# A feed-forward's first output part by block products, with modulation rows moved and the mixer's end list-scheduled

## The chip, the cores and the metric

The kernel runs on one core of one Trainium2 chip. The metric is the device time of one execution in microseconds (us). The runs of the kernel before took 983.15, 978.13 and 983.17 us, a median of 983.15.

## The reference

One decoder layer over 512 tokens of width 1024, in float32. Nine vectors of 1024 values (shift, scale and gate for each of three sub-layers) are made from a conditioning vector: `mod = silu(c) @ w_ada + b_ada`. Then:

```python
u = modulate(rmsnorm(h, g_norm_ffn1), sh1, sc1)
h = h + 0.5 * gt1 * swiglu(u, w_ffn1_in, w_ffn1_out)
u = modulate(rmsnorm(h, g_norm_mix), sh2, sc2)
h = h + gt2 * token_mixing(u, ...)
u = modulate(rmsnorm(h, g_norm_ffn2), sh3, sc3)
h = h + 0.5 * gt3 * swiglu(u, w_ffn2_in, w_ffn2_out)
out = rmsnorm(h, g_final)
```

`swiglu(u, w_in, w_out)` is `(silu(u @ w_a) * (u @ w_b)) @ w_out` with an inner width of 2816, that is 22 tiles of 128. `token_mixing` projects `u`, pools and attends, and ends with `merged = sigmoid(gates_1) * (y_pool @ w_pb) + sigmoid(gates_2) * (y_attn @ w_ab)` and `merged @ w_out`.

## The kernel before

**Precision.** Each float32 matrix product is made of three matmuls on a pair of float32r tiles, a leading part and a remainder (`mm3`): hi x hi, hi x lo, lo x hi. Leading parts are made by ScalarE (a copy), remainders by VectorE (a subtraction). This holds for activations (`UH`/`UL`, `HI`/`HK`) and for weights: every weight chunk of 128 x 1024 is loaded by SP into a raw buffer, and `split_hi` and `split_lo` write it into the rings `whi` and `wlo`, some chunks ahead of its use (`look`, `take`). For chunks in the set `added`, the remainder is made by ScalarE (a negated copy) and an adding DMA issued by GpSimd, and VectorE is spared.

**Layout.** Tokens are columns, 512 of them (`T`, half of it `HT`); features are tiles of 128 rows. The residual is `H[0..7]`.

**Feed-forward.** The 22 inner tiles are worked in five parts, `PARTS = ((0, 4), (4, 8), (8, 12), (12, 16), (16, 22))`. For each part the inner activations of its tiles are made, and then the part's share of the output is added to `H`. An inner tile is made in one of two ways. *Plain* (`ffn_pair`): two tiles of 24 matmuls of 512 columns (one for `a`, one for `b`), a silu and a product. *By blocks* (`duo`): two inner tiles at once, as a 2 x 2 block product with seven products instead of eight (Winograd's form of Strassen's scheme); each product is 24 matmuls of 256 columns. The output of a part has the same two ways: plain, 8 tiles of 4 x 3 matmuls of 512 columns; or by `out_block`, seven products of 24 matmuls of 256 columns. For `out_block` the activations of four inner tiles are needed as seven blocks: `split_a` splits two blocks that are there, `split_s` makes four sums of 256 columns and splits them. Of a part's four output chunks, three more weight blocks are sums; VectorE (`make`) and GpSimd (`sum`, an adding DMA) make them in the buffers `X`.

`BLOCKED = (1, 2, 3)` says for which parts the output is by `out_block`, in both feed-forwards. In the second one (`ffn2`) pairs 0 to 3 are plain (`PLAIN[2] = 4`): two in `head`, beside the norm, two behind it. Then comes part 0's plain output, then part by part two duos and an output block.

**Modulation rows.** One row is a column of `mod` for 128 features: SP loads 512 KB of `wada`, and VectorE multiplies by the condition and sums (`ada_do`). `bg()` does one row and starts the next load. Rows 56 to 63 run in the mixer's output loop, rows 64 to 71 (half of the last gate) in the second feed-forward, from its head to pair 3, with the buffers `cs` and `AR`.

**Order.** Between `begin()` and `end()` the calls go to a `Recorder`. `flush` then issues them: TensorE's in the written order, those of the other engines, SP and GpSimd included, by a list schedule with estimated costs and due times. Both feed-forwards are recorded. The mixer is not: its calls are issued as written, the gates (`gate_duo`), the branches (`branch`) and the output loop of `merge_out` and its tail (`out_tail`) included. In the gates' blocks, `branch`'s `merge` and `parts` wait in the list `rest` and are put by hand between the products.

**Lines.** Recorded instructions all carry line 320 (`flush`). Written ones carry their own: 521 and 538 the weight splits, 599 the rows, 664 to 674 the norm's statistics and their spread, 681 to 707 the norm, 730 and 731 the tail.

Of the kernel before, what the change touches and what calls it, by code (L numbers as in the profile page):

```python
# [14 lines left out]
P = 128  # L15
# [3 lines left out]
KT = 8  # L19
# [50 lines left out]
def lay_ffn(w_in, w_out, first, plain):  # L70
# [3 lines left out]
    ins, outs = [], []  # L74
# [62 lines left out]
BLOCKED = (1, 2, 3)  # L137
ADDED = {0: (0,), 2: (0, 3, 5)}
# [185 lines left out]
class Kernel:  # L324
# [6 lines left out]
    def plan(self):  # L331
# [52 lines left out]
        def ffn(n, ins, outs, first):  # L384
# [4 lines left out]
            for part, (k0, k1) in enumerate(PARTS):  # L389
                recs = outs[part * KT // 2:(part + 1) * KT // 2] if part + 1 < len(PARTS) else outs[-KT:]  # L390
                while j < pairs_before(n, part):
# [5 lines left out]
                    else:  # L397
                        own = part in BLOCKED and j + 2 == PARTS[part][1]
                        blocks(ins[at:at + 4], recs if own else None, ADDED[n] if own else ())
# [18 lines left out]
        self.fetched = self.done = self.made = 0  # L418

# [197 lines left out]
    def bg(self):  # L617
# [8 lines left out]
        if self.ada_next > 64:  # L626
            if k % 2 == 0:
                self.ada_fin("half", self.ada_next - 2, self.ada_next)
        elif k == 0:
# [256 lines left out]
    def plain_of(self, j):  # L886

        k0, k1 = next(x for i, x in enumerate(PARTS) if x[0] <= j < x[1] and i not in BLOCKED)
# [11 lines left out]
    def blocked(self, j):  # L900
        return any(PARTS[i][0] <= j < PARTS[i][1] for i in BLOCKED)
# [16 lines left out]
    def block(self, j, i0, i1):  # L918

        d = (j - next(PARTS[i][0] for i in BLOCKED if PARTS[i][0] <= j < PARTS[i][1])) // 2  # L920
# [169 lines left out]
    def out_block(self, n, k0, last, hooks):  # L1090
# [80 lines left out]
    def ffn2(self):  # L1171
# [50 lines left out]
    def ffn(self, n, j, last=None):  # L1222
# [9 lines left out]
        for part, (k0, k1) in enumerate(PARTS):  # L1232
            tail = part + 1 == len(PARTS)
            extra = int(part - 1 not in BLOCKED)
            while j < pairs_before(n, part):
# [3 lines left out]
                else:  # L1239
                    own = part in BLOCKED and j + 2 == k1  # L1240
# [5 lines left out]
            if part in BLOCKED:  # L1246
# [84 lines left out]
    def mix_sums(self, x, slots):  # L1331
# [20 lines left out]
        def last():  # L1352
            u = x[3].rearrange("p (k t) -> p k t", k=4)
            nc.scalar.activation(self.S[3][0], u, AF.Copy)
            sub(self.S[3][1], u, self.S[3][0])
# [254 lines left out]
    def mix(self):  # L1610
# [12 lines left out]
        with tc.tile_pool(name="rt", bufs=1) as self.rt, tc.tile_pool(name="aw", bufs=2) as self.aw, \  # L1623
# [149 lines left out]
            sig = lambda i: lambda: nc.scalar.activation(at[i], gates[i], AF.Sigmoid)  # L1773
            gates.append(self.mm_tile({1: [nxt, sig(0)], 2: [sig(1)], 4: [lambda: self.at_spread(spread)]}))
            self.YH, self.YL = two("YH"), two("YL")
            self.at_y(spread)
            gates.append(self.mm_tile({1: [sig(2)]}))
            sig(3)()
            assert not sums
        self.merge_out(at, last, ma)  # L1780
        outer.close()

    def gate_duo(self, s, c, p5, last, rest):
# [11 lines left out]
        for i, (bank, u, start) in enumerate(((A, lambda: blk(lo4, T1), True), (B, lambda: S(0), True),  # L1795
# [6 lines left out]
            if not i:  # L1802
                rest(2)
            self.product(bank, u(), start, not i)
            if i == 0:
                copy(C, A)
                if last:
                    last()
            elif i == 1:
                copy(p5, B)  # L1810
                rest()
# [11 lines left out]
    def merge_out(self, ready, last, ma):  # L1823
        nc, tc = self.nc, self.tc
        v = nc.vector
        with tc.tile_pool(name="mg", bufs=1) as mg:
# [15 lines left out]
            def branch(m):  # L1842
# [3 lines left out]
                if rest:  # L1846
                    do()
                w = self.take()
# [312 lines left out]
```

## Time and profile before

| | us |
|---|---|
| runs (median) | 983.15 (978.13 to 983.17) |
| the profiled execution | 977.58 |
| its span, first to last instruction | 975.7 |
| TensorE busy | 964.1 |
| VectorE busy | 800.7 |
| ScalarE busy | 545.8 |
| GpSimd busy | 91.1 |

In the rows of the profile, PE is TensorE (PEld its weight loads), DVE VectorE, ACT ScalarE, POOL GpSimd, and SP the engine that issues most loads. A row of the table by stretches gives a stretch, its length, and for each engine the busy time and the number of instructions in it; then the granted clock of TensorE, the busy share of the DMA engines and GB/s. A row of the timeline gives start, duration, engine, line, operation, what it writes and reads, and in brackets how long the engine stood before it and what ended that. A row of the groups gives the number of instructions, their sum and the mean in ns, and the engine's idle time before them. A row of the waits gives who waited for whom, the sum, how often, and the longest.

### The profile page before, as it was taken

To read this page: it belongs to the slowest core of one execution; us is meant where nothing else is said; L and a number is where in the kernel's file an instruction comes from. 1 tells how busy PE (TensorE), PEld (TensorE's weight loads), DVE (VectorE), ACT (ScalarE), POOL (GpSimd) and SP (SyncE) were. 2 spreads that over 40 slices of the span, in tenths; PEclk is the share of its full clock that TensorE was granted. 3 is DMA by queue.
4 is the path that set the end of the run, shared out by engine and by line. 5 is a ranking of instruction groups with operands and counts; after the bars stand their busy time and mean duration, and the time that the engine had idled before them with its cause. 6 is when DMAs were issued, how large, how long until landed. Compare 5 with 4: busy or idle time off the path is not lost.

```text
span 975.7 us, 17744 instructions
## 1 busy us (share of the span) xinstructions
PE 964.1 (99%) x7114; PEld 898.4 (92%) x7114; DVE 800.7 (82%) x1209; ACT 545.8 (56%) x821; POOL 91.1 (9%) x102
## 2 busy tenths in 40 slices
PE   8999999999999999999999999999999999999997
PEld 7888999999999999788879998998899999999997
DVE  7989999999997577898877767797677979888653
ACT  5463666657566353455555552465376576676553
POOL 0000111101010000007200000001111121110002
PEclk9999999999999999999999999999999999999999
DMA  9868768788887217654246536558668787796602
GB/s 349 282 222 269 206 181 200 226 231 225 214 215 198 87 46 241 202 187 139 82 122 166 152 95 225 165 165 248 162 149 230 176 199 198 173 218 180 167 1 87
DMA packets 55109, 177.49 MB, mean 182 GB/s; under 512 B 7409, under 2 KB 10225, under 8 KB 55026
## 3 DMA queue, kind: packets, MB, share of 16 engines
q1 hardware_dynamic: 44224, 140.18, 44.7%
q0 software_dynamic: 10224, 35.66, 19.7%
q8 instruction: 55, 0.90, 0.4%
q10 hardware_dynamic: 578, 0.53, 0.2%
q14 instruction: 28, 0.23, 0.1%
HBM read 135.29 MB, written 2.24 MB: 141 GB/s over the span
## 4 chain that ended last, share of the span: by engine, by line
PE 93%; DMA 2%; DVE 1%; SPq 1%; ACT 1%; issue 1%; POOL 0%; POOLq 0%; DVEq 0%; ACTq 0%
PE bank L320 58%; PE bank L568 7%; PE bank L569 6%; PE bank L570 6%; PE bank L1016 2%; PE bank L1018 2%; PE bank L1017 2%; PE bank L2082 2%; PE bank L2084 1%; PE bank L2086 1%; DMA raw<-wf2i 1%; SPq L1413 1%; PE bank L1757 1%; PE bank L1459 1%; PE bank L1510 1%
## 5 line engine op out<-in xcount | busy, mean ns | idle before, releaser
L320 PE MATMUL bank<-UH,whi 128*128 128x256 f32 (+2 forms) x674 | 193.2, 287 | 0.0
L320 PE MATMUL bank<-UL,whi 128*128 128x256 f32 (+1 forms) x672 | 193.0, 287 | 0.1
L320 PE MATMUL bank<-UH,wlo 128*128 128x256 f32 (+1 forms) x672 | 192.7, 287 | 0.0
L320 DVE TENSOR_TENSOR wlo<-X,whi 128x1024 fp32r<-128x1024 f32 (+2 forms) x114 | 130.9, 1161 | 17.0 <-ACT whi L320 16.8
L320 PE MATMUL bank<-HK,whi 128*128 128x256 f32 (+1 forms) x472 | 140.6, 298 | 1.2 <-DVE HK L320 1.2
L320 PE MATMUL bank<-HI,wlo 128*128 128x256 f32 (+1 forms) x472 | 140.6, 298 | 0.0
L320 PE MATMUL bank<-HI,whi 128*128 128x256 f32 (+2 forms) x473 | 140.6, 298 | 0.0
L320 ACT ACTIVATE whi<-X 128x1024 fp32r<-128x1024 f32 (+3 forms) x119 | 118.2, 1010 | 34.9 <-DVE X L320 20.8
L320 PEld LDWEIGHTS bank<-UH,whi 128*128 128x128 f32 x674 | 126.5, 188 | 2.6
L320 PEld LDWEIGHTS bank<-UL,whi 128*128 128x128 f32 x672 | 126.2, 188 | 2.8 <-DVE UL L707 0.3
L320 PEld LDWEIGHTS bank<-UH,wlo 128*128 128x128 f32 x672 | 126.2, 188 | 2.5
L320 PE MATMUL bank<-SH,whi 128*128 128x256 f32 x408 | 112.6, 276 | 0.0
L320 PE MATMUL bank<-SL,whi 128*128 128x256 f32 x408 | 112.6, 276 | 0.0
L320 PE MATMUL bank<-SH,wlo 128*128 128x256 f32 x408 | 112.6, 276 | 0.0
L320 ACT ACTIVATE whi<-raw 128x1024 fp32r<-128x1024 f32 (+3 forms) x99 | 83.7, 857 | 45.4 <-PE bank L320 36.5
L320 PEld LDWEIGHTS bank<-HK,whi 128*128 128x128 f32 x472 | 88.6, 188 | 5.2 <-DVE HK L320 1.8
L320 DVE TENSOR_TENSOR wlo<-raw,whi 128x1024 fp32r<-128x1024 f32 (+3 forms) x85 | 81.7, 972 | 12.8 <-ACT whi L320 12.2
L320 PEld LDWEIGHTS bank<-HI,wlo 128*128 128x128 f32 x472 | 88.6, 188 | 3.9 <-DVE wlo L320 0.2
L320 PEld LDWEIGHTS bank<-HI,whi 128*128 128x128 f32 x473 | 88.8, 188 | 3.5
L538 DVE TENSOR_TENSOR wlo<-raw,whi 128x1024 fp32r<-128x1024 f32 (+4 forms) x65 | 71.2, 1109 | 16.1 <-ACT whi L521 16.0
L320 PEld LDWEIGHTS bank<-SH,wlo 128*128 128x128 f32 x408 | 76.6, 188 | 0.0
L320 PEld LDWEIGHTS bank<-SL,whi 128*128 128x128 f32 x408 | 76.6, 188 | 0.0
(377 smaller groups left out, 2242.1 us busy)
## 6 DMA issues: line engine op xcount, KB each, us to landing
raw<-wmix SPq DMA_DIRECT2D x44, 512.0 KB, 3.9
raw<-wf1i SPq DMA_DIRECT2D x29, 512.0 KB, 5.6
raw<-wf2i SPq DMA_DIRECT2D x29, 512.0 KB, 4.3
AR<-wada SPq DMA_DIRECT2D x23, 512.0 KB, 5.0
X<-X POOLq DMA_DIRECT2D x22, 512.0 KB, 5.1
cs<-wada SPq DMA_DIRECT2D x16, 512.0 KB, 4.5
raw<-raw POOLq DMA_DIRECT2D x16, 512.0 KB, 5.8
ada<-wada SPq DMA_DIRECT2D x15, 512.0 KB, 5.7
```

Source lines behind the costliest of these rows:

```text
L320: getattr(self.real[eng], method)(*a, **k)
L538: self.nc.vector.tensor_tensor(self.lo[:, y], r[:, x], self.hi[:, y], op=OP.subtract)
L568: M(ps, hi, uh, start=start, stop=False)
L569: M(ps, hi, ul, start=False, stop=False)
L570: M(ps, lo, uh, start=False, stop=stop)
L1016: M(o, hi, uh, start=start and p == 0 and k == 0, stop=False, skip_group_check=True)
L1017: M(o, hi, ul, start=False, stop=False, skip_group_check=True)
L1018: M(o, lo, uh, start=False, stop=k == 3, skip_group_check=True)
L1413: nc.sync.dma_start(w[32 * o:32 * o + 32], t[32 * i:32 * i + 32])
L1459: nc.tensor.matmul(S[:, o], q[:, toks], k[:, ks], start=True, stop=True, skip_group_check=True)
L1510: self.nc.tensor.matmul(self.bO[64 * h:64 * h + 64, P * hp:P * hp + P], x, pt[:, (2 * h + j) * P:(2 * h + j + 1) * P], start=j == first, s ...
L2082: M(b, hi, self.UH[k], start=k == 0, stop=False)
```

## The change

Four things. Part 0's output in the second feed-forward is made by `out_block`: its chunks are laid out as blocks, one of the seven weight remainders (`ALONE`) goes by the adding DMA, and pairs 0 to 3 are split as blocks. The sums of the inputs (`u_steps`) are recorded together, right behind the head, and the raw buffers that they hold are freed there (`more`). The rows move one stage up: rows 56 to 63 into the gates, with one buffer made of the `ut` tiles, rows 64 to 71 into the mixer's output loop, with three. And the mixer's end, from its fourth gate tile to the tail, is recorded and issued by the list schedule, in three pieces.

```diff
-BLOCKED = (1, 2, 3)
-ADDED = {0: (0,), 2: (0, 3, 5)}
+BLOCKED = {0: (1, 2, 3), 2: (0, 1, 2, 3)}
+ALONE = (3,)
+ADDED = {0: ((0,),) * 3, 2: ((),) + ((0, 3, 5),) * 3}
...
-                if part not in BLOCKED:
-                    if n and part + 1 < len(PARTS):
-                        self.added.update(range(len(self.order), len(self.order) + KT // 2))
+                if part not in BLOCKED[n]:
                     plain(recs)
+                elif PARTS[part][1] <= PLAIN[n]:
+                    blocks(recs, added=ALONE)
...
@@ def out_block(self, n, k0, last, hooks, extra=0)
             w[0] = self.take()
+            if extra:
+                self.settle(A[0], w[0][0][0], u[0][0][0])
...
@@ def ffn2(self)
-        self.ada_free, self.ada_stop, self.ada_depth = [self.cs, self.AR], 72, 2
-        self.bg_fetch()
+        self.blk = BLOCKED[2]
         adds, (s2, s1, s0, last) = self.u_steps(2)
-        self.todo = adds[:3] + [s0[0], adds[3], s0[1], s2[0], adds[4], s2[1], s1[0], adds[5], s1[1]]
-        do = lambda n: [self.todo.pop(0)() for _ in range(n)]
+        for f in adds + s0 + s2 + s1:
+            f()
+        self.more()
         for j in range(2):
             self.ffn_post(j, self.ffn_silu(j, bk[2 * j]), bk[2 * j + 1])
-            do((2, 3)[j])
-            self.bg()
-        pa = self.ffn_tile()
-        do(len(self.todo))
-        self.bg()
-        self.ffn_post(2, self.ffn_silu(2, pa), self.ffn_tile())
-        self.bg()
-        self.ffn_pair(3, self.bg)
-        self.todo = [self.bg, self.bg, self.more]
-        self.ffn(2, 4, lambda: [f() for f in last])
+        self.todo = []
+        self.ffn(2, 2, lambda: [f() for f in last])
...
@@ def ffn(self, n, j, last=None)
-            extra = int(part - 1 not in BLOCKED)
+            extra = int(not part or part - 1 not in self.blk)
...
-            if part in BLOCKED:
+            if part in self.blk:
+                if k1 <= PLAIN[n]:
+                    old = [self.banks[(self.bi + i) % 6] for i in range(6)]
+                    out = self.out_block(n, k0, (old[5], old[3], old[4]), self.todo, 1)
+                    out[0]()
+                    out[1](lambda: None)
                 continue
...
@@ def gate_duo(self, s, c, p5, last)
             self.look(4)
-            if not i:
-                rest(2)
+            if i in (3, 6):
+                self.bg()
             self.product(bank, u(), start, not i)
...
@@ def merge_out(self, ready, last, ma, before)
+            self.before = dict.fromkeys(("PE", "POOL", "SP", "DMA"), 0.) | {"DVE": 3000., "ACT": 1000.}
+            self.begin()
+            before()
+            self.ada_free, self.ada_stop = [self.utv[:, :D]], 64
+            self.bg_fetch()
             for j in MERGED[::2]:
                 if j < 6:
...
-                    self.gate_duo(*sc, p5, last, do)
-                    last = None
+                    self.gate_duo(*sc, p5, last)
+                    last = lambda: None
+                    if j != 2:
+                        self.end()
+                        if j:
+                            place(tile_of(ma, "v23", 4), 4, 5)
+                            rows = [ma.tile([P, D], F32, name=x) for x in ("k0", "k2", "v1")]
+                        else:
+                            for i, t in enumerate(("q2", "q1", "k1")):
+                                place(tile_of(ma, t), i + 1)
+                        self.begin()
                 for m in (j, j + 1):
...
                     branch(m)
+                    do(2)
+            assert self.ada_next == 64 and not self.adat, self.ada_next
             self.ready = False
-            self.ada_free, self.ada_stop, self.ada_depth = [ma.tile([P, D], F32, name=x) for x in ("k0", "k2", "v1")], 64, 2
+            self.ada_free, self.ada_stop, self.ada_depth = rows, 72, 3
             self.bg_fetch()
...
             self.out_tail((5, 6, 7), ks, gate, 2, lambda m: sc[m % 2][:, m // 6 * T:(m // 6 + 1) * T])
+            self.end()
...
-        self.uts = [tl(f"ut{i}", T) for i in range(3)]
+        self.utv = tl("ut", 3 * T)
+        self.uts = [self.utv[:, i * T:(i + 1) * T] for i in range(3)]
```

In `branch`, rows are also begun at the tiles 0 and 2 (`if m in (0, 2): self.bg()`). The six other rows of the gates are begun before the products 3 and 6 of the three gate blocks. `before()` is the fourth gate tile and its sigmoids, which stood ahead of `merge_out`.

More of the change, by code (lines that the diff above doesn't have):

```diff
@@ L67, in _out_blocks, with lay_ffn @@
                            axis=1) for i, j in ((0, 0), (0, 1), (1, 1), (1, 0))]
-def lay_ffn(w_in, w_out, first, plain):
-    ins, outs = [], []
+def lay_ffn(w_in, w_out, n, first):
+    ins, outs, plain = [], [], PLAIN[n]
     if first:
@@ L886, in plain_of @@
     def plain_of(self, j):
-        k0, k1 = next(x for i, x in enumerate(PARTS) if x[0] <= j < x[1] and i not in BLOCKED)
+        k0, k1 = next(x for i, x in enumerate(PARTS) if x[0] <= j < x[1] and i not in self.blk)
         x = slice(NB + (j - k0) * T if k1 < FT else (j - k0) * T, NB + (j - k0 + 1) * T if k1 < FT else (j - k0 + 1) * T)
@@ L918, in block @@
     def block(self, j, i0, i1):
-        d = (j - next(PARTS[i][0] for i in BLOCKED if PARTS[i][0] <= j < PARTS[i][1])) // 2
+        d = (j - next(PARTS[i][0] for i in self.blk if PARTS[i][0] <= j < PARTS[i][1])) // 2
         x = slice(d * NB + i0 * HT, d * NB + i1 * HT)
@@ L1239, in ffn @@
                 else:
-                    own = part in BLOCKED and j + 2 == k1
+                    own = part in self.blk and j + 2 == k1
                     if own and n == 0:
@@ L1776, in mix, with before, gate_duo @@
             self.at_y(spread)
+            assert not sums
+        def before():
             gates.append(self.mm_tile({1: [sig(2)]}))
             sig(3)()
-            assert not sums
-        self.merge_out(at, last, ma)
+        self.merge_out(at, last, ma, before)
         outer.close()
-    def gate_duo(self, s, c, p5, last, rest):
+    def gate_duo(self, s, c, p5, last):
         nc, v = self.nc, self.nc.vector
@@ L1821, in gate_duo, with merge_out @@
         nc.scalar.activation(c, c, AF.Sigmoid, scale=-1.0)
-    def merge_out(self, ready, last, ma):
-        nc, tc = self.nc, self.tc
-        v = nc.vector
+    def merge_out(self, ready, last, ma, before):
+        tc = self.tc
         with tc.tile_pool(name="mg", bufs=1) as mg:
@@ L1914, in merge_out @@
                 add()
-            assert self.ada_next == 64 and not self.adat, self.ada_next
+            assert self.ada_next == 72 and not self.adat, self.ada_next
             self.ada_free = None
```

52 lines of the change are left out of this document (22 added, 30 removed).

## The prediction

> **What bounds the kernel now.** I read the page first: the busy shares and the chain that ended last.
>
> ```profile
> span 975.7 us, 17744 instructions
> ...
> PE 964.1 (99%) x7114; PEld 898.4 (92%) x7114; DVE 800.7 (82%) x1209; ACT 545.8 (56%) x821; POOL 91.1 (9%) x102
> ...
> PE 93%; DMA 2%; DVE 1%; SPq 1%; ACT 1%; issue 1%; POOL 0%; POOLq 0%; DVEq 0%; ACTq 0%
> ```
>
> TensorE is busy 964.1 of 975.7 us and makes 93% of the chain. Time can be won in two ways only: fewer matmul columns, or less of the 11.6 us (975.7 - 964.1) in which TensorE stands. Next come the stages, from the table by stretches. I cut it where the kind of matmul changes: three output blocks of the first feed-forward, the mixer's gates, then the second feed-forward: head, pairs 2 and 3, output of part 0, and by turns two duos and an output block.
>
> ```profile
> core 0: us, PE busy (x) PEld busy (x) DVE busy (x) ACT busy (x) POOL busy (x), PEclk, DMA share, GB/s
> 122.25:141.54 19.29, 19.29 (x171) 19.14 (x169) 18.88 (x32) 11.86 (x18) 1.73 (x2) 1.00 0.78 211
> 179.62:198.91 19.29, 19.29 (x170) 19.13 (x169) 19.06 (x28) 12.77 (x19) 1.75 (x2) 1.00 0.72 202
> 236.99:256.27 19.28, 19.28 (x170) 19.13 (x169) 18.66 (x27) 13.74 (x21) 1.76 (x2) 1.00 0.75 209
> 505.00:582.00 77.00, 77.00 (x589) 73.38 (x588) 57.63 (x70) 43.12 (x61) 5.24 (x6) 1.00 0.53 134
> 633.44:657.83 24.39, 23.43 (x202) 22.97 (x201) 23.98 (x49) 15.82 (x31) 0.00 (x0) 1.00 0.56 171
> 657.83:679.62 21.79, 21.79 (x99) 18.03 (x97) 16.62 (x30) 12.91 (x17) 2.61 (x3) 1.00 0.90 255
> 679.62:701.38 21.76, 21.76 (x98) 18.03 (x97) 16.97 (x23) 7.83 (x9) 1.73 (x2) 1.00 0.57 155
> 701.49:739.58 38.09, 38.09 (x339) 38.09 (x338) 25.49 (x30) 23.10 (x33) 6.11 (x7) 1.00 0.72 180
> 739.58:758.62 19.04, 19.04 (x171) 19.04 (x170) 16.31 (x24) 14.63 (x21) 2.60 (x3) 1.00 0.89 213
> ...
> 796.70:817.79 21.09, 19.88 (x171) 19.29 (x169) 16.25 (x24) 15.60 (x22) 3.79 (x5) 1.00 0.87 202
> ...
> 855.87:874.91 19.04, 19.04 (x171) 19.04 (x169) 17.17 (x25) 14.79 (x21) 2.58 (x3) 1.00 0.95 227
> ```
>
> To see: the granted clock is 1.00 throughout. An output part by plain products takes 21.76 us, one by block products 19.04, or 19.29 where VectorE is full (first feed-forward: 18.66 to 19.06 us busy of 19.29). (A stretch also counts the two or three matmuls that reach in over its edge: 96 start in the plain part, 168 in a block part.) In the gates, 77 us, TensorE never stands and VectorE has 19.4 us free. Last I asked for TensorE's waits over the whole span, and for the instructions around the two that lie behind the gates.
>
> ```profile
> PE bank L320 <- DVE HK L320: 1.2, 2, 1.0
> PE bank L1983 <- DVE ones L1988: 1.1, 1, 1.1
> PE bank L320 <- DVE r L320: 0.9, 1, 0.9
> ```
>
> ```profile
> 630.85 1.22 DVE L538 TENSOR_TENSOR wlo<-raw,whi 128x1024 fp32r<-128x1024 f32 x1
> 631.98 0.86 DVE L681 SCALAR_TENSOR_TENSOR ut<-H,mod,bank 128x256 f32<-128x256 f32 x2
> ...
> 636.68 2.08 ACT L320 ACTIVATE whi<-raw 128x1024 fp32r<-128x1024 f32 x3
> ...
> 639.60 1.22 DVE L320 TENSOR_TENSOR wlo<-raw,whi 128x1024 fp32r<-128x1024 f32 x1
> 640.73 0.16 DVE L320 RECIPROCAL r<-r 128x2 f32<-128x2 f32 x1
> ...
> 797.09 0.61 ACT L320 ACTIVATE HI<-hf 128x512 fp32r<-128x512 f32 x1
> ...
> 798.23 1.23 DVE L320 TENSOR_TENSOR X<-raw,raw 128x1024 f32<-128x1024 f32 x1 [1.28 <-DMA raw<-wf2i]
> 799.37 0.68 DVE L320 TENSOR_TENSOR hf<-hf,bank 128x512 f32<-128x512 f32 x1
> 799.97 0.68 DVE L320 TENSOR_TENSOR HK<-hf,HI 128x512 fp32r<-128x512 f32 x1
> ...
> 801.70 0.42 DVE L320 SCALAR_TENSOR_TENSOR hf<-hf 128x256 f32<-128x256 f32 x1
> 802.04 0.42 DVE L320 TENSOR_TENSOR HK<-hf,HI 128x256 fp32r<-128x256 f32 x1
> 803.25 1.22 DVE L320 TENSOR_TENSOR HK<-hf,HI 128x1024 fp32r<-128x1024 f32 x1 [0.79 <-ACT HI L320]
> ```
>
> The wait for `r` is in the head of the second feed-forward: the reciprocal stood behind a weight remainder of 1.22 us on VectorE, and that chain's ScalarE step behind three weight copies. The wait for `HK` is in part 2's output block: VectorE stood for a late transfer, and the activations' remainders queued behind it. The third wait is at the start.
>
> **The change part by part.** *Products of part 0.* Plain: 8 output tiles x 4 inner tiles x 3 matmuls = 96 of 512 columns, 21.76/96 = 0.227 us each. By blocks: 7 products x 24 = 168 of 256 columns, 19.04/168 = 0.113 us each, so half the width costs half the time. The settling matmul of 240 columns moves from part 1's first duo into this block: nothing. The gain is 21.76 - 19.04 = 2.72 us at most, 21.76 - 19.29 = 2.47 where VectorE is full. I take **-2.5** for the reason in the next part; the worse bound is the worst block shown, 21.09: -0.7.
>
> The trace decides here between two formulas of the Trainium skill, page "TensorE: Matmul & The Clock Gate", section "Back-to-back issue gap". Its formula for one matmul (columns / 2.4 ns + 2.5) gives 0.109 and 0.216 us, an estimated gain of 2.4 us. Its sustained spacing, 81 ns at 128 columns and 131 ns at 512, would instead make halving the width costly. The rows above (0.227 and 0.113) side with the first.
>
> *VectorE's work in 633.44 to 701.38.* It is busy 23.98 + 16.62 + 16.97 = 57.6 of 67.9 us. Prices:
>
> ```profile
> L320 DVE SCALAR_TENSOR_TENSOR H<-bank,mod,H 128x512 f32<-128x512 f32 x7 | 5.2, 749 | 3.6 <-PE bank L320 3.6
> L320 DVE SCALAR_TENSOR_TENSOR cs<-cs,cond 128x1024 f32<-128x1024 f32 x4 | 4.9, 1220 | 2.8 <-DMA cs<-wada 2.8
> L320 DVE SCALAR_TENSOR_TENSOR AR<-AR,cond 128x1024 f32<-128x1024 f32 x4 | 4.9, 1219 | 2.4 <-DMA AR<-wada 2.4
> L320 DVE TENSOR_TENSOR wlo<-X,whi 128x1024 fp32r<-128x1024 f32 x3 | 3.6, 1217 | 0.0
> L320 DVE TENSOR_TENSOR HK<-hf,HI 128x512 fp32r<-128x512 f32 x4 | 2.7, 685 | 0.7 <-ACT HI L320 0.7
> L320 DVE TENSOR_TENSOR X<-raw,raw 128x1024 f32<-128x1024 f32 x1 | 1.2, 1212 | 0.0
> L320 DVE TENSOR_SCALAR ng<-mod 128x2 f32<-128x2 f32 x4 | 0.7, 168 | 0.1
> ```
>
> Out go the eight modulation rows, 8 x 1.22 = 9.8, and some twelve small operations at 0.17, 2.0: 11.8 us. In come six weight remainders, 6 x 1.22 = 7.3 (before, all four chunks' were formed by ScalarE and an adding DMA; now one of seven is); two weight sums, 2 x 1.21 = 2.4; for each of two pairs of tiles four sums of 0.42 and remainders of 0.42, 1.22 and 0.69 in place of two of 0.69, +2.6 each, 5.3; and the block's updates, eight of 256 columns at 0.42, four sums at 0.68, four updates at 0.75, 9.1 against 8 x 0.75 = 6.0: +3.1. That is +18.1 - 11.8 = +6.3: 63.9 us of work in a stretch of 67.9 - 2.5 = 65.4. What does not fit can go into the next two duos, where VectorE is free for 38.09 - 25.49 = 12.6 us. The three blocks of the first feed-forward, with VectorE as full and likewise one remainder in seven given to the DMA, lose only 0.25 us each; hence 19.29 above. Without that cover the 6.3 us would lie on the path.
>
> *The start of the block.* Its first 24 products need only pairs 0 and 1: 24 x 0.113 = 2.7 us. Behind them stands what pair 3 leaves: its product by the silu and its split, 0.68 + 0.61 + 0.68 = 2.0 us. The remainders of the sums, in part 2 at 799.37 (product) to 804.47, come 5.1 us after that product's start, here some 0.7 later for pair 3's own remainder, 5.8 us; they are needed after 48 matmuls and the three of the third product that read pairs 0 and 1, and a settling one, 52 x 0.113 = 5.9 us. It just fits: 0, bounds 0 and +1.2 (one weight remainder wrongly ahead).
>
> *ScalarE, GpSimd, transfers.* ScalarE makes 7 + 1 weight copies in place of 4 + 4, and eight copies of results (8 x 0.61 = 4.9 us, by the row of 797.09) beside 7.83 us busy of 21.76. GpSimd issues three adding DMAs in place of four. SP loads the same weight bytes; eight row transfers of 512 KB leave a stretch that has a DMA share of 0.90 and 0.57. Spare raw buffers come free earlier. No cost; if weights came late it would look like part 2's wait, 2.05 us.
>
> *Rows in the mixer.* The last eight rows now run in the mixer's output loop, where the eight before them ran; those go into the gates: 8 x 1.22 = 9.8 us of VectorE into 19.4 free, leaving 9.6, and 4 MB at a DMA share of 0.53. They share one buffer, so each row's load waits on SP until VectorE has consumed the row before, and the weight loads issued later queue behind it; TensorE feels it only if the wait outlasts the chunks already split ahead (about four, at 24 x 0.113 = 2.7 us each for a gate product). 0, bounds 0 and +2.
>
> *The mixer's end by the list schedule.* TensorE's order there is kept, and it has no wait to lose before 633. What can be gained is the head's: 24.39 us for 192 matmuls at 0.1133 (21.75) and eight small ones (about 0.7) is 1.9 us lost, by weight work ahead of the statistics on VectorE and ScalarE. Half of that chain is issued by the part that is now scheduled (630.85 delays the first norms by 1.2 us), and two rows of 1.22 leave the head. I take **-1.2**, bounds -1.9 and +1.
>
> *Part 2's wait* (21.09 - 19.04 = 2.05): the work from part 1 on is the same, so I leave it: 0, bounds -2.05 and +2.
>
> **The sum:** -2.5 - 1.2 = -3.7 us. The profiled execution took 977.58 us (span 975.7 and 1.9 around it), so it would take 973.9. It lies 5.6 under the median of the runs shown, 983.15 (978.13 to 983.17); from the median the forecast is **979.4**. The runs themselves spread by 5 us, 0.5%, about what a measurement of this kernel can tell from no change.
>
> **Rivals.**
>
> A. *Both waits go*: -2.7 - 1.9 - 2.05 = -6.7, 976.5 us. For it: five of six output blocks have no such wait, and the late transfer behind it may fall elsewhere once the stretch shifts. Against: the order of its VectorE instructions and its loads are not touched.
>
> B. *The gain is eaten*: the block costs as much as part 2's (21.09), the head keeps its 1.9 us, and one more wait of a remainder, 1.2 us, appears: -0.7 + 1.2 = +0.5, 983.7 us. For it: 63.9 of 65.4 us is 98% of VectorE. Against: the 12.6 us behind it.
>
> C. *VectorE becomes the bound (slower)*. In 633 to 701 it was idle 67.9 - 57.6 = 10.3 us, waiting for banks, copies and rows. If it cannot use that idle time and hands nothing on, the stretch takes 63.9 + 10.3 = 74.2 us, +6.3: 989.4. It is slower by over 0.5% once the idle time that stays exceeds 67.9 + 4.9 - 63.9 = 8.9 us. Against: 5.2 us of that idle time was waiting for the rows, which leave.
>
> D. *Halving the width does not halve the time*: by a straight line through the two sustained points a product of 256 columns takes more than half of one of 512. As a mechanism of this kernel: the weight load, 188 ns for each matmul whatever its width, would then bound the block at 168 x 0.188 = 31.6 us, +9.8, 993 us. Against: 168 already fit in 19.04 here, so the loads overlap.
>
> ```profile
> L320 PEld LDWEIGHTS bank<-HK,whi 128*128 128x128 f32 x472 | 88.6, 188 | 5.2 <-DVE HK L320 1.8
> ```
>
> The page's sustained spacing, named above, is what speaks for D.
>
> **How the numbers follow.** The forecast (-2 to -4.9 us) 0.52, A 0.22, B 0.14, C 0.11, D 0.01. The run spread of 5 us moves a third of the forecast's chance over the bound on the fast side. Faster by over 0.5%: 0.19 + 0.16 of A + 0.02 of B = 0.37; slower: 0.09 of C, 0.01 of D and 0.02 of B = 0.12; the same: 0.51. The range goes from A less 3.5 for a run like the faster one, 973, to 985, between B and C. The forecast's own range is 974 to 981.
>
> **What would show it.** Right: part 0's output in about 19.1 to 19.3 us; the head under 23.5; no new TensorE wait in the gates; VectorE nearly full from 658 to 699. Wrong: a wait for `HK` or `wlo` at part 0's block or the duo behind it; TensorE waiting in the gates behind a row's load; the head still at 24.4; part 2's wait gone or doubled.

## The result, and the profile after

The changed kernel took 973.25 us, the median of 12 runs (970.41 to 978.08); the kernel before, run beside it, 979.18 us, the median of 12 (975.3 to 983.17). The ratio is 0.9938, interval 0.9918 to 0.9957: 6.1 us faster, interval 4.2 to 8.0. The profiled execution took 973.68 us (span 971.9), 3.9 us less than the one before (977.58, span 975.7). Two runs of one kernel below, the one with the products undone, were disturbed (995.22 and 997.11 us at a granted clock of 0.95); its ratio leaves them out, and its profile is one of them.

The page of the changed kernel, in the lines shown of before (its recorded instructions carry line 321):

```profile
span 971.9 us, 17908 instructions
...
PE 963.3 (99%) x7186; PEld 902.3 (93%) x7186; DVE 815.3 (84%) x1229; ACT 551.7 (57%) x828; POOL 87.7 (9%) x98
...
PE 94%; DVE 1%; issue 1%; DMA 1%; ACT 1%; SPq 0%; POOL 0%; POOLq 0%; ACTq 0%; DVEq 0%
```

TensorE's busy time fell by only 0.8 us, its idle time from 11.6 to 8.6. Neither number says where the gain is. The stretches do. The same table for the changed kernel, cut at the same changes of the matmuls: part 4 of the first feed-forward, which lies behind its three output blocks (the second fence has it for the kernel before), the gates, then the head, pairs 2 and 3, part 0's output block, and by turns two duos and an output block.

```profile
core 0: us, PE busy (x) PEld busy (x) DVE busy (x) ACT busy (x) POOL busy (x), PEclk, DMA share, GB/s
255.71:315.07 59.36, 59.36 (x506) 59.36 (x505) 50.68 (x63) 35.34 (x48) 4.34 (x5) 1.00 0.73 198
507.00:584.00 77.00, 76.80 (x581) 72.97 (x580) 66.88 (x89) 43.31 (x61) 5.25 (x6) 1.00 0.74 212
636.35:659.25 22.90, 22.90 (x202) 22.90 (x201) 22.90 (x43) 16.79 (x32) 0.00 (x0) 1.00 0.24 70
659.25:681.03 21.78, 21.78 (x98) 18.03 (x97) 18.87 (x24) 13.43 (x18) 2.61 (x3) 1.00 0.69 162
681.03:700.20 19.17, 19.17 (x171) 19.16 (x169) 16.90 (x23) 13.13 (x19) 1.73 (x2) 1.00 0.62 172
700.20:738.28 38.08, 38.08 (x339) 38.08 (x338) 30.50 (x40) 22.70 (x31) 5.25 (x6) 1.00 0.70 171
738.28:757.32 19.04, 19.04 (x171) 19.04 (x170) 16.48 (x24) 14.26 (x21) 2.60 (x3) 1.00 0.87 213
...
795.40:814.44 19.04, 19.04 (x171) 19.04 (x170) 18.16 (x26) 13.95 (x21) 2.62 (x3) 1.00 0.73 198
...
852.52:871.56 19.04, 19.04 (x171) 19.04 (x170) 17.96 (x26) 14.89 (x22) 2.61 (x3) 1.00 0.82 201
```

```profile
256.27:313.39 57.12, 57.12 (x506) 57.12 (x505) 50.69 (x63) 35.38 (x48) 4.33 (x5) 1.00 0.80 211
```

Three stretches got shorter and one longer:

| stretch | before, us | after, us | difference |
|---|---|---|---|
| part 0's output (and a settling matmul) | 21.87 (679.62 to 701.49) | 19.17 | -2.70 |
| head of the second feed-forward | 24.39 | 22.90 | -1.49 |
| part 2's output block | 21.09 | 19.04 | -2.05 |
| first feed-forward, part 4 | 57.12 | 59.36 | +2.24 |

Together -4.0, and the span fell by 3.8. The last row was not in any forecast: the same 504 matmuls, in a place that the change does not touch, at the same granted clock of 1.00 and without a wait in the stretch, took 4% longer. The section on the spacing comes back to it.

TensorE's waits in the changed kernel (what it waited for: us in total, times, longest):

```profile
PE bank L1995 <- DVE ones L2000: 1.1, 1, 1.1
PE bank L1457 <- DVE k L1420: 0.6, 1, 0.6
PE bank L2094 <- ACT UH L692: 0.5, 1, 0.5
PE bank L321 <- ACT bank L321: 0.2, 1, 0.2
PE bank L663 <- ACT ut L730: 0.2, 1, 0.2
```

Both waits that the prediction had found behind the gates, for `r` (0.9) and for `HK` (1.2), are gone.

### The profile page after: what moved, and what is told of

Same layout as the page of the kernel before. It is cut to its first block, busy times and chain, and to the rows that moved or that the text cites. A ratio compares the mean times of both kernels' runs of the same rounds, so it can differ in the third digit from the quotient of the medians.

```text
span 971.9 us, 17908 instructions
## 1 busy us (share of the span) xinstructions
PE 963.3 (99%) x7186; PEld 902.3 (93%) x7186; DVE 815.3 (84%) x1229; ACT 551.7 (57%) x828; POOL 87.7 (9%) x98
## 3 DMA queue, kind: packets, MB, share of 16 engines
HBM read 135.29 MB, written 2.24 MB: 142 GB/s over the span
## 4 chain that ended last, share of the span: by engine, by line
PE 94%; DVE 1%; issue 1%; DMA 1%; ACT 1%; SPq 0%; POOL 0%; POOLq 0%; ACTq 0%; DVEq 0%
PE bank L321 71%; PE bank L570 4%; PE bank L572 4%; PE bank L571 4%; PE bank L2094 2%; PE bank L2098 1%; PE bank L2096 1%; PE bank L1755 1%; PE bank L1457 1%; DMA ut<-wada 1%; PE bank L1508 1%; PE bank L1756 1%; PE bank L1757 1%; PE bank L1490 1%; PE bank L2029 0%
## 5 line engine op out<-in xcount | busy, mean ns | idle before, releaser
L321 PE MATMUL bank<-UH,whi 128*128 128x256 f32 (+1 forms) x780 | 223.6, 287 | 0.0
L321 PE MATMUL bank<-UL,whi 128*128 128x256 f32 (+1 forms) x776 | 223.0, 287 | 0.0
L321 PE MATMUL bank<-UH,wlo 128*128 128x256 f32 (+1 forms) x776 | 223.0, 287 | 0.0
L321 DVE TENSOR_TENSOR wlo<-X,whi 128x1024 fp32r<-128x1024 f32 (+2 forms) x117 | 135.8, 1172 | 18.4 <-ACT whi L321 17.9
L321 PEld LDWEIGHTS bank<-UH,whi 128*128 128x128 f32 x780 | 146.5, 188 | 3.1
L321 PEld LDWEIGHTS bank<-UH,wlo 128*128 128x128 f32 x776 | 146.1, 188 | 2.8
L321 PEld LDWEIGHTS bank<-UL,whi 128*128 128x128 f32 x776 | 145.7, 188 | 2.8
L321 ACT ACTIVATE whi<-raw 128x1024 fp32r<-128x1024 f32 (+3 forms) x125 | 107.3, 876 | 44.9 <-PE bank L321 39.0
L321 DVE TENSOR_TENSOR wlo<-raw,whi 128x1024 fp32r<-128x1024 f32 (+3 forms) x117 | 113.3, 983 | 13.2 <-ACT whi L321 12.7
L321 PEld LDWEIGHTS bank<-SH,whi 128*128 128x128 f32 x408 | 76.6, 188 | 0.0
```

What stands on the lines that cost most here:

```text
L321: getattr(self.real[eng], method)(*a, **k)
```

## The experiments

The change has three parts: the block products of part 0 (called B here), the rows moved into the gates (R) and the mixer's end by the list schedule (L). A ratio is to the kernel before, on the same chip.

**One part undone.**

*Products undone: part 0 plain again, rows and schedule as changed.*

```
-BLOCKED = {0: (1, 2, 3), 2: (0, 1, 2, 3)}
+BLOCKED = {0: (1, 2, 3), 2: (1, 2, 3)}
...
+                    if n and part + 1 < len(PARTS):
+                        self.added.update(range(len(self.order), len(self.order) + KT // 2))
```

> The changed kernel with part 0's output of the second feed-forward plain again (rows moved and mixer's end list-scheduled as in the change). Theory P (the products give 2.6 us, the two waits are another matter): part 0's output takes 21.8 us in place of 19.2, the head stays under 23.2 us, part 2's block stays at 19.04; some 2.6 us slower than the changed kernel, 0.9965 of the kernel before. Theory W (part 2's wait left because part 0's block form shifted the weight loads): part 2's block shows 20 to 21 us again; 0.998 to 1.000 of the kernel before.

Measured: 976.6 us, ratio 0.9966 (0.9944 to 0.9988). From its profile only the stretch of 512 columns is read:

```profile
690.42:712.18 21.76, 21.76 (x97) 18.02 (x96) 16.64 (x19) 5.86 (x7) 1.94 (x3) 0.95 0.72 183
```

Part 0's output takes 21.76 us again (the same in the profiles of the schedule alone and of the rows alone, below), and the whole lies 2.7 us above the changed kernel by the two ratios (the intervals alone leave about 3 either way; the stretch is what carries it). So the saved columns are paid in full. Whether the block is what removed the wait at part 2 is read from the schedule alone and the rows alone, which have part 0 plain too: neither has the wait, so the block is not needed for it to go.

*Rows undone: rows 64 to 71 in the second feed-forward again, from behind the head on.*

```
@@ ffn2
+        self.ada_free, self.ada_stop, self.ada_depth = [self.cs, self.AR], 72, 2
+        self.bg_fetch()
...
             self.ffn_post(j, self.ffn_silu(j, bk[2 * j]), bk[2 * j + 1])
+            self.bg()
+            self.bg()
@@ beside (pairs 2 and 3)
+            self.bg()
@@ gate_duo, branch, merge_out
-            if i in (3, 6):
-                self.bg()
...
-                if m in (0, 2):
-                    self.bg()
...
-            self.ada_free, self.ada_stop, self.ada_depth = rows, 72, 3
+            self.ada_free, self.ada_stop, self.ada_depth = rows, 64, 2
```

> The changed kernel with the modulation rows where they were before (56 to 63 in the mixer's output loop, 64 to 71 in the second feed-forward, from the head's end to pair 3). Theory L (the list schedule frees the head): head under 23.4 us; VectorE has about 11.8 us more work in the stretch from the head to part 0's end than the 58.7 of 63.9 us it has now, so some of it goes on the path: 1 to 4 us in part 0's block and the duos behind it, 0.995 to 0.998 of the kernel before. Theory R (the rows' leaving freed the head): head back at 24 us or more. If VectorE bounds outright: 6 us or more, at or over 1.000.

Measured: 978.21 us, ratio 0.9989 (0.9966 to 1.0012). Nearly all of the gain is lost, some 5 us, more than the 1 to 4 expected. The head stays at 22.90 us, as Theory L had it, and part 0's block costs no more than in the changed kernel (19.16 us with its settling matmul). The table by stretches shows where: part 1's block, the two duos behind it, part 2's block.

```profile
739.43:759.03 19.60, 19.60 (x171) 19.60 (x170) 16.73 (x24) 15.40 (x22) 3.48 (x4) 1.00 0.89 213
759.03:798.60 39.57, 39.57 (x339) 39.57 (x337) 33.49 (x43) 24.02 (x34) 6.10 (x7) 1.00 0.71 176
798.60:818.39 19.79, 19.79 (x171) 19.79 (x170) 17.60 (x25) 14.60 (x21) 2.62 (x3) 1.00 0.93 213
```

TensorE does not stand in any of them; it is slower. 336 matmuls of two duos take 39.57 us instead of 38.08, that is 117.8 ns from start to start instead of 113.3. The trace has the moment at which this begins. The timeline of the kernel with the rows undone, ScalarE (ACT), VectorE (DVE), weight loads (PEld) and matmuls (PE), with start, duration and operation of each:

```profile
741.95 1.05 ACT L321 ACTIVATE whi<-X 128x1024 fp32r<-128x1024 f32 x1
...
742.64 1.22 DVE L321 TENSOR_TENSOR wlo<-X,whi 128x1024 fp32r<-128x1024 f32 x1
742.91 1.04 ACT L321 ACTIVATE HI<-hf 128x1024 fp32r<-128x1024 f32 x1
...
743.98 1.23 DVE L321 TENSOR_TENSOR HK<-hf,HI 128x1024 fp32r<-128x1024 f32 x1
...
745.10 0.19 PEld L321 LDWEIGHTS bank<-HI,whi 128*128 128x128 f32 x1
...
745.21 0.28 PE L321 MATMUL bank<-HI,whi 128*128 128x256 f32 x1
745.26 0.19 PEld L321 LDWEIGHTS bank<-HK,whi 128*128 128x128 f32 x1
745.32 0.32 PE L321 MATMUL bank<-HK,whi 128*128 128x256 f32 x1
...
745.48 0.28 PE L321 MATMUL bank<-HI,wlo 128*128 128x256 f32 x1
...
745.60 0.28 PE L321 MATMUL bank<-HI,whi 128*128 128x256 f32 x1
...
745.72 0.28 PE L321 MATMUL bank<-HK,whi 128*128 128x256 f32 x1
```

Weight work stands ahead of the activations on both engines: on VectorE a remainder (742.64, ends at 743.86) ahead of the sums' remainder `HK`, on ScalarE a weight copy (741.95) ahead of the leading part `HI` that `HK` needs. `HI` ends last, at 743.95, and `HK` starts behind it and ends at 745.21; the load that needs it was due there and starts at 745.26, 0.05 us late. Before it the matmuls start 0.11 us apart, behind it 0.12, and they keep that spacing until 869.4 us, through some 1,050 matmuls: 4.7 us in all. There a late weight remainder (0.2 us) ends it, and a second one in the same block, at 875.0 us, costs 0.6 us more. In the changed kernel no weight work stands at these places, and `HK` begins 4.1 us after the block's start (738.28) instead of 4.6 (739.43). Its timeline on the two engines:

```profile
741.27 1.06 ACT L321 ACTIVATE HI<-hf 128x1024 fp32r<-128x1024 f32 x1 [0.47 <-DVE hf L321]
...
742.36 1.23 DVE L321 TENSOR_TENSOR HK<-hf,HI 128x1024 fp32r<-128x1024 f32 x1 [0.79 <-ACT HI L321]
```

*Schedule undone: the mixer's end in the order written by hand, with the rows in it.* `mix`, `gate_duo` and `merge_out` are those of before, and to them come:

```
@@ gate_duo
+            if i in (3, 6):
+                self.bg()
@@ branch
+                if m in (0, 2):
+                    self.bg()
@@ merge_out
+            self.ada_free, self.ada_stop = [self.utv[:, :D]], 64
```

> The changed kernel with the mixer's end issued by hand as before (its rows moved as in the change, placed before the same products). Theory L: the head is at 24.0 to 24.5 us again, 1.3 us slower than the changed kernel; rows in the gates without a list schedule cost 0 to 2 us more. Theory R: head under 23.2 us, as fast as the changed kernel. Part 0's block 19.1 to 19.3 us under both.

Measured: 974.14 us, ratio 0.995 (0.9928 to 0.9972), 1.2 us above the changed kernel by the two ratios, about what Theory L had. The head of its second feed-forward, in the table by stretches:

```profile
640.33:664.72 24.39, 23.43 (x203) 22.98 (x201) 23.98 (x45) 17.06 (x32) 0.00 (x0) 1.00 0.28 84
```

24.39 us again, with the wait of 0.9 us for `r`, although two rows less stand in it. So the rows that leave do not free the head. What does shows on VectorE in the changed kernel:

```profile
641.03 1.22 DVE L321 TENSOR_TENSOR wlo<-raw,whi 128x1024 fp32r<-128x1024 f32 x1
642.16 0.16 DVE L321 RECIPROCAL r<-r 128x2 f32<-128x2 f32 x1
```

The reciprocal still stands behind a weight remainder, but it starts 5.8 us after the head's start (636.35), where before it was 7.3 (640.73, 633.44): the chain ahead of it begins earlier.

**One part alone.**

*Products alone.* Only the block products of part 0; `mix`, `gate_duo` and `merge_out` are those of before, and the rows run as in the kernel with the rows undone.

```
-BLOCKED = (1, 2, 3)
+BLOCKED = {0: (1, 2, 3), 2: (0, 1, 2, 3)}
```

> The block products of part 0 alone: mixer's end by hand and the rows where they were before. Theory L and the count of VectorE's work (57.6 + 18.1 = 75.7 us in a stretch of 65): head 24.4 us or more, part 0's block and the duos behind it wait 2 to 6 us in all, 0.998 to 1.003 of the kernel before. If VectorE's work can be put off (12.6 us free in the next two duos): part 0's block at 19.3, 0.997.

Measured: 977.97 us, ratio 0.9978 (0.9951 to 1.0005). Head 24.38 us, part 0's block 19.05; and from 744.2 to 868.3 us the slow spacing again, behind the same order on ScalarE and VectorE, by its timeline:

```profile
740.84 1.05 ACT L321 ACTIVATE whi<-X 128x1024 fp32r<-128x1024 f32 x1
...
741.52 1.22 DVE L321 TENSOR_TENSOR wlo<-X,whi 128x1024 fp32r<-128x1024 f32 x1
741.79 1.05 ACT L321 ACTIVATE HI<-hf 128x1024 fp32r<-128x1024 f32 x1
...
742.87 1.23 DVE L321 TENSOR_TENSOR HK<-hf,HI 128x1024 fp32r<-128x1024 f32 x1
```

2.7 us are won at part 0, 4.7 lost behind part 1. With part 2's wait gone here too (1.5 us, see below) and part 3's block late as in the kernel with the rows undone (0.8), the stretches make 1.3 us of loss, and the profiled span is 1.8 longer than that of the kernel before (977.5 against 975.7); the medians say 2.2 of gain (4.8 of gain to 0.5 of loss). The two do not meet. Single profiles differ by slow stretches elsewhere, and this kernel has only one, so its account stays open.

*Schedule alone.* The kernel with the rows undone, and part 0 plain too (its remainders as in the kernel with the products undone).

```
-BLOCKED = {0: (1, 2, 3), 2: (0, 1, 2, 3)}
+BLOCKED = {0: (1, 2, 3), 2: (1, 2, 3)}
```

> The mixer's end by the list schedule alone: part 0's output plain, the rows where they were before. Theory L: head under 23.4 us in place of 24.4, 1.0 to 1.5 us faster than the kernel before, 0.9985. Theory R (the rows do it): head 24.0 or more, 1.000.

Measured: 975.47 us, ratio 0.9959 (0.9935 to 0.9984). Its head in the table by stretches:

```profile
635.28:658.18 22.90, 22.90 (x203) 22.90 (x201) 22.90 (x45) 16.83 (x32) 0.00 (x0) 1.00 0.42 128
```

The head takes 22.90 us with two rows still behind it: the list schedule alone frees it. Part 2's block is at 19.04 here too, which is why the gain is larger than the 1.0 to 1.5 us expected.

*Rows alone.* The kernel with the schedule undone, and part 0 plain too (its remainders likewise).

```
-BLOCKED = {0: (1, 2, 3), 2: (0, 1, 2, 3)}
+BLOCKED = {0: (1, 2, 3), 2: (1, 2, 3)}
```

> The moved rows alone: part 0's output plain, the mixer's end issued by hand. Theory R': the rows' leaving takes the late remainders (and the slower spacing that follows them) out of the second feed-forward: parts 1 to 4 all at 113.3 ns with no wait, 2 to 3 us faster than the kernel before, 0.997 to 0.998; head still 24.4. Otherwise 1.000.

Measured: 977.06 us, ratio 0.9982 (0.9961 to 1.0003). Its head in the table by stretches:

```profile
635.45:659.84 24.39, 23.39 (x202) 22.93 (x201) 23.98 (x45) 17.07 (x32) 0.00 (x0) 1.00 0.26 85
```

The head stays at 24.39; part 2's block is at 19.04, without its wait. The gain is about what Theory R' had, but by a wait that went: the kernel before has no slow stretch in the second feed-forward that could leave.

By the ratios (times 979.18) the parts are worth, in us: B -2.2, R -1.8, L -4.0; B and L -1.1; B and R -4.9; L and R -3.3; all three -6.1. Each has some 2 us of uncertainty either way. They do not add up, for two reasons. Each part alone takes out the same wait at part 2, which counts once in a sum. And from part 1's block of the second feed-forward on, the slow spacing is in both kernels that have B without R, and in neither of those with both.

**The spacing itself.** What switches it? The kernels have a settling matmul of 240 columns wherever matmuls of 512 columns give way to 256. Three kernels put more of them in.

*One settling matmul at the start of parts 1 to 4 of the second feed-forward, on the kernel with the rows undone.*

```
-            extra = int(not part or part - 1 not in self.blk)
+            extra = int(n == 2 or not part or part - 1 not in self.blk)
```

> The changed kernel with its rows where they were before (as in the run before), and one settling matmul of 240 columns (0.11 us) more at the first duo of each of parts 1 to 4 of the second feed-forward. There, a wait of 0.05 us at 745 us was followed by a spacing of 117.8 ns in place of 113.3 up to 869 us, 5 us in all, with no further wait. Theory S (a matmul rhythm that any late start can upset and a settling matmul restores): the stretches from the first duo of part 2 on are back at 113.3 ns, 3 to 4.5 us faster than without it, 0.994 to 0.996 of the kernel before. Theory D (the spacing is the weights' or VectorE's supply, rows or no rows): still 117.8, 0.999. Theory X: a settling matmul inside a stream of 256 columns upsets it itself: more stretches at 117.8, over 1.000.

Measured: 977.74 us, ratio 0.9987 (0.9965 to 1.0008): no gain. The spacing does not stay at 113.3; it changes sides at each settling matmul, the first of them at a place where it was fast: duos of 39.57, 38.10 and 39.57 us, part 4 57.14.

*One settling matmul at the start of every part, in both feed-forwards, on the changed kernel.*

```
-            extra = int(not part or part - 1 not in self.blk)
+            extra = 1
```

> The changed kernel with a settling matmul at the first duo of every part of both feed-forwards (six more, 0.65 us). Its profile showed 2.2 us lost to the slower spacing in the first feed-forward. Theory S: all feed-forward duos at 113.3 ns, spread of the runs narrower, 1 to 2 us faster than the changed kernel, 0.992 of the kernel before. Theory D: 0.65 us slower than the changed kernel, 0.9945.

Measured: 981.39 us, ratio 1.0017 (0.9998 to 1.0036), that is some 8 us above the changed kernel for seven matmuls of 0.11 us (the edit makes seven, not the six of the expectation). Its three stretches of two duos in the second feed-forward:

```profile
702.76:742.34 39.58, 39.58 (x339) 39.58 (x337) 30.55 (x40) 22.99 (x31) 5.25 (x6) 1.00 0.66 165
762.24:800.34 38.10, 38.10 (x339) 38.10 (x337) 31.47 (x42) 25.41 (x35) 5.19 (x6) 1.00 0.75 189
819.49:859.06 39.57, 39.57 (x338) 39.57 (x337) 30.81 (x40) 25.02 (x34) 5.19 (x6) 1.00 0.73 183
```

Slow, fast, slow, with no late operand in this feed-forward. So the spacing does not depend on VectorE's load, and one extra matmul switches it. The 8 us are accounted for: its two feed-forwards have four slow stretches of 500 matmuls at 2.2 us each, where the changed kernel's profile has one; the head takes 0.6 us more (23.53), and the seven matmuls 0.8.

*Two settling matmuls in a row at the same seven places.*

```
-        if extra:
+        for _ in range(extra):
             self.settle(...)
...
+            extra = 1 if not part or part - 1 not in self.blk else 2
```

> The changed kernel with two settling matmuls in a row (0.22 us) at the first duo of parts 2 to 4 of the first and of parts 1 to 4 of the second feed-forward, seven places, 14 matmuls, 1.5 us. One settling matmul at these places moved the spacing from 113.3 to 117.8 ns and the next one back again, and cost 8 us in all. Theory T (each odd matmul switches between the two spacings): two in a row leave it where it is; the second feed-forward stays at 113.3 ns throughout, 1.5 us slower than the changed kernel, 0.995 to 0.996 of the kernel before. Theory U (any such matmul inside a stream upsets it): stretches at 117.8 again, 1.001.

Measured: 974.97 us, ratio 0.9954 (0.9925 to 0.9983), as Theory T had it. Twice as many extra matmuls, some 6 us less time, and the same three stretches:

```profile
697.70:735.79 38.09, 38.09 (x339) 38.09 (x337) 30.20 (x40) 22.92 (x31) 5.25 (x6) 1.00 0.70 170
755.05:793.13 38.08, 38.08 (x338) 38.08 (x337) 31.84 (x42) 25.50 (x35) 5.20 (x6) 1.00 0.77 191
812.40:850.48 38.08, 38.08 (x338) 38.08 (x337) 30.40 (x40) 24.52 (x33) 5.18 (x6) 1.00 0.75 185
```

One switches the spacing, two leave it: single settling matmuls switched it at all eleven places of the two kernels, and pairs left it at all seven. Pairs were tried at the fast spacing only.

*The slow stretch of the changed kernel's first feed-forward.* It begins behind a late operand too. The changed kernel, in part 3's output block, with the last two weight loads and the matmul of the second:

```profile
252.68 0.19 PEld L321 LDWEIGHTS bank<-HK,whi 128*128 128x128 f32 x1
...
253.01 0.19 PEld L321 LDWEIGHTS bank<-HI,wlo 128*128 128x128 f32 x1
253.02 0.38 PE L321 MATMUL bank<-HI,wlo 128*128 128x256 f32 x1
```

The load for a weight remainder was due 0.11 us after the one before it, at 252.79, and starts 0.22 us late; the matmul is shown as longer (0.38), not as a wait. Each of the first feed-forward's three output blocks shows this lateness, which is most of the 0.25 us that the prediction found these blocks to lose. What follows differs: in the ten profiles at a granted clock of 1.00 that have no added settling matmuls, it comes 28 times at the fast spacing, which stays 23 times and turns slow 5 times. So a late operand can switch the spacing and mostly does not. Part 1's block of the second feed-forward, 0.05 us late, switched in both profiles that have it; the late loads for `HK` at part 2 switched in none of the three profiles of the kernel before. What decides is open.

**More profiles of the two kernels**, unchanged, for what varies from one execution to the next: the kernel before twice, the changed one once.

> The kernel before, once more, for its waits. If the wait at part 2's output block belongs to the kernel: again 1 to 2 us at about 800 us. If it belongs to the one execution: none. The head at 24.4 us in either case.

> As the run before: the wait at part 2's output block again, or not; the head at 24.4 us; the stretches at 117.8 ns in other places than in the first profile.

> The changed kernel, once more. Waits of the second feed-forward: none over 0.3 us, head under 23.2 us; in the gates again the wait of about 0.4 us at 572 us if it belongs to the kernel; the stretch at 117.8 ns of the first feed-forward elsewhere or absent if it belongs to the execution.

Measured, in the order of the expectations: 977.89, 979.5 and 972.25 us. The heads are 24.39, 24.39 and 22.91 us. Part 2's block in the table by stretches, first in the one and then in the other execution of the kernel before:

```profile
798.22:817.92 19.70, 19.62 (x171) 19.23 (x169) 16.02 (x23) 15.19 (x22) 3.39 (x4) 1.00 0.91 213
```

```profile
799.01:819.82 20.81, 19.89 (x171) 19.30 (x169) 16.34 (x24) 15.67 (x22) 3.87 (x5) 1.00 0.87 202
```

With the 21.09 of the prediction's profile, taken first, the loss there against 19.04 is 2.05, 0.66 and 1.77 us: part of the kernel before in all three, 1.5 on the mean. (In the first of the two the view of waits names none for `HK`; loads for it start late there too, and the matmuls count as busy.) The second of them also ran part 4 of the first feed-forward at the slow spacing (59.36 us), the first did not; the changed kernel did in the profile shown above and did not in the new one (57.12).

Why the wait is gone shows on VectorE. The timeline of the kernel before, second execution, at the start of part 2's block, and then that of the changed kernel in its first profile:

```profile
800.25 1.22 DVE L320 TENSOR_TENSOR X<-raw,raw 128x1024 f32<-128x1024 f32 x1 [0.91 <-DMA raw<-wf2i]
801.39 0.68 DVE L320 TENSOR_TENSOR hf<-hf,bank 128x512 f32<-128x512 f32 x1
```

```profile
795.60 0.69 DVE L321 TENSOR_TENSOR hf<-hf,bank 128x512 f32<-128x512 f32 x1 [0.53 <-PE bank L321]
...
801.23 1.22 DVE L321 TENSOR_TENSOR X<-raw,raw 128x1024 f32<-128x1024 f32 x1
```

Before, the sum of two weight chunks stands ahead of the activations' chain and holds it until its transfer has landed; after, it stands behind it. The order costs time even without a late transfer: in the first further execution the sum starts at 798.34, 0.12 us after the block's start, and the block still loses 0.66. The schedule emits the order of the whole second feed-forward at once, and each of the three parts, alone, changed it here: in none of the kernels with any part of the change does TensorE wait for `HK` at part 2. No run moves that one sum alone, and why the schedule's costs tip that way stays open.

## Why the prediction was right, and where it was off

The forecast was a gain of 3.7 us, on a median of 983.15: 979.4. The longer series put the kernel before at 979.18, so the same gain would have meant 975.5, and the measured gain is 6.1. The median of 973.25 lies outside the forecast's own range (974 to 981) and 0.25 us inside the lower end of the whole range (973 to 985): the sign was right, the size too small by 2.4 us and the base 4.0 too high, and that it lies inside is owed to the width. The other figure, 973.9 from the profile, comes close to the profiled 973.68 by luck: a wait of 2.05 us that went and a stretch that took 2.24 longer, neither forecast, cancel there.

*What can change the time.* The prediction allows two ways only, "fewer matmul columns, or less of the 11.6 us". There is a third, on which the experiments turned: the same matmuls at another spacing, with TensorE counted as busy.

*Products: -2.5 predicted, -2.7 measured* (21.87 to 19.17, each with its settling matmul). Half the width costs half the time, and rival D is out: the Trainium skill's one-matmul formula (page "TensorE: Matmul & The Clock Gate", section "Back-to-back issue gap") fits within 5% at the fast spacing (0.109 against 0.113, 0.216 against 0.227), its sustained spacing does not fit.

*VectorE: 63.9 us predicted from 633 to 701.* In the changed kernel it is busy 22.90 + 18.87 + 16.90 = 58.7 us in that stretch, and the duos behind it went from 25.49 to 30.50: 5.0 us were handed on, 63.7 together. The overflow was paid out of idle time, as forecast, and the block ran at the 19.05 of a block without a wait.

*The start of the block: it just fits, 0.* Right for part 0. The margin of 0.1 us that was worked out for it, 5.9 against 5.8, has its twin at part 1: there the kernels with the block and without the rows' move miss it by 0.05 us.

*Rows in the gates: 0.* VectorE went from 57.63 to 66.88 us of the 77 (67.4 were to be expected), and TensorE lost 0.2 us there (76.80). In the further profile of the changed kernel nothing is lost. No load of a row held TensorE.

*The mixer's end by the list schedule: -1.2 predicted, -1.49 measured.* Of the two causes named, the schedule is the one: alone it gives 22.90, the rows alone leave 24.39. The prediction blamed two things, a weight remainder ahead of the reciprocal and one ahead of the first norms; the first still stands there in the changed kernel, and only the start of the chain has moved.

*Part 2's wait: 0 predicted, -1.5 measured on the mean, -2.05 against the prediction's own profile.* This is the step that failed. "The work from part 1 on is the same, so I leave it", and of rival A, "the order of its VectorE instructions and its loads are not touched": the code of part 2 is not touched, but its order is no property of that code. Rival A had the outcome, both waits gone, at a chance of 0.22, and with -6.7 us also the nearer size; its reason was a transfer that falls elsewhere, and the traces show another order on VectorE.

*Rival C* supposed that VectorE would become the bound, at +6.3 us. In the full change it does not. In the kernels with the block and with the rows left beside it, the loss is of another kind: not time in which TensorE stands, but one remainder 0.05 us late, behind weight work on ScalarE and VectorE, and 4.7 us of slower spacing behind it. Rival B did not come: no wait was added at part 0, and the head was freed. The prediction costed the rows' move at nothing, rightly for the gates; its worth, 5 us once the block is there (0.9989 against 0.9938), it did not see.

The sum of what the stretches show: -2.7 - 1.5 - 1.5 = -5.7, against 6.1 measured (4.2 to 8.0). What is left, 0.4 us, is within the interval; and of either kernel one profile has part 4 of the first feed-forward at the slow spacing, 2.2 us, and another has not.

## What to carry to other kernels

When a schedule emits the order of a whole stage, any edit in the stage may reorder all of it: cost a wait elsewhere in the stage as one that may go or come, not at zero. A small lateness on the operand of a long run of equal matmuls may cost its own length or, where the spacing switches, far more: look at the spacing from start to start behind it, since the view of waits and the busy time do not show it. And read a part's worth together with its companions: the rows' move won nothing in the head and yet decided whether the products' gain was kept.

## What the runs showed of the hardware

Matmuls of 256 columns with a weight load each run at one of two spacings, 113.3 or 117.8 ns, for a whole stretch, at a granted clock of 1.00 in both; TensorE is counted as busy all the time, and no wait is shown. The price is 1.5 us for two duos, 0.75 for an output block, 2.2 for part 4 of the first feed-forward. Matmuls of 512 columns took 0.227 us in every profile. One extra matmul of 240 columns inside a stream of 256 switched it at 11 places of 11, two in a row left it at 7 of 7 (from the fast side), and behind the one at the change from 512 to 256 columns it was fast. One operand 0.05 us late switched it in 2 profiles of 2, one 0.22 us late at 5 places of 28. What in TensorE has these two states no run here shows.
